# Moving the weight tiles of an fp32r transformer trunk to another SBUF offset

## The chip, the cores and the metric

The kernel runs on one core of one Trainium2 chip. The metric is device time in microseconds. Times of several executions are given as their median. The profile comes from one execution of its own.

## The reference

The reference computes a trunk of two layers on 256 tokens with 1024 features, all in float32. Cut to what matters:

```python
for i in range(DEPTH):                                    # DEPTH = 2
    x = x + 0.5 * swiglu(rms_norm(x, ffn1_norm_g[i]), ffn1_w_in[i], ffn1_w_out[i])
    hn = rms_norm(x, mix_norm_g[i])
    if i % 2 == 0:                                        # mixer 0: mLSTM heads
        proj = hn @ a_w_in[0]
        y_tok = mlstm_heads(proj[..., :A_TOK], a_gate_b[0], a_h_norm_g[0])
    else:                                                 # mixer 1: sliding-window heads
        proj = hn @ b_w_in[0]
        y_tok = swa_heads(proj[..., :B_TOK], cos, sin, ...)
    y_mem = memory_heads(proj[..., TOK:], mem_k, mem_v, ...)   # cross-attention to 256 memory rows
    x = x + concat([y_tok, y_mem], -1) @ w_out
    x = x + 0.5 * swiglu(rms_norm(x, ffn2_norm_g[i]), ffn2_w_in[i], ffn2_w_out[i])

def swiglu(x, w_in, w_out):                               # hidden width 2816
    gate, up = jnp.split(x @ w_in, 2, axis=-1)
    return (jax.nn.silu(gate) * up) @ w_out
```

Before the layers, memory keys and values are computed as `rms_norm(mem) @ mem_w_kv`. So there are four feed-forward blocks, two mixers and a memory part; nearly all arithmetic is in products with weight matrices.

## The kernel before

Activations are kept transposed, features on the 128 partitions and the 256 tokens along a row. Each weight matrix is read once from HBM in tiles of 128 partitions by 1024 float32 values (`wtile`: pool `wrp`, tile `wr`, 5 buffers, issued on the SyncE queue). For the precision, each operand is split into a part rounded to fp32r and the rest: ScalarE writes the rounded part of the weights (`wh`, pool `whp`, 8 buffers), VectorE the rest (`wl`, pool `wlp`, 8 buffers). The split activations are the tiles `xh` and `xl` (pools `xhp`, `xlp`, 4 buffers each, two feature chunks per tile, written by `Norm.put`) for a norm's output, and tiles `u` (pool `up`) for hidden units, head outputs and the memory rows. The helper `mm3` (lines 227 to 229) makes one product out of three matmuls, high by high, high by low and low by high, all added up in one PSUM bank.

There are two arrangements. In the feed-forward blocks (`ffn_in`, `ffn`), in the output projections of the mixers (`out_proj`) and in a part of the first mixer's input projection, a 128x128 piece of a weight tile stands in the array (it is loaded by an LDWEIGHTS, the profile's engine PEld) and 256 columns of activations move through it. In groups with `rows=True` (the memory part, six groups of the first mixer and all seven of the second) it is the other way round: 128 columns of an activation tile stand and 256 columns of a weight tile move. The memory part also has a first stretch of its own (`first_part`, line 357). Every matmul is preceded by its own load.

Which tile of a pool is used next, and at which address each pool lies, follows from the order in which the pools are made: pools are placed one after another along each partition's row of SBUF, and a pool's size shifts all that come after it. A tile's begin modulo 512 bytes is called its residue here. The pieces within a tile lie 512 or 1024 bytes apart, so a whole tile has one residue. In the built program before:

| tiles | first address | residue |
|---|---|---|
| kT, vM (memory keys, values) | 20416 | 448 |
| xh, xl | 29120, 37312 | 448 |
| u | 45504 | 448 |
| wr, wh, wl | 113152, 133632, 166400 | 0 |
| t (scratch) | 199168 | 0 |
| acc | 218368 | 256 |
| onesr (constant, for the sums of a norm) | 16512 | 128 |

The order of the work on TensorE and on the SyncE queue is written out by hand: generators for the main chain and for the side chains of norms and heads are woven by the class `Weave` by a table of expected delays (`LAT`), and only these two engines are kept to that order. The other engines are scheduled by the framework. `memory()` starts with 18 matmuls on a zeroed scratch tile, while the first transfers are under way.

The five norms are made in `program()`. `x1` feeds the first mixer, `x4` the second; `x0`, `x2`, `x3` and `x5` feed the feed-forward blocks. `x4` is the only one all of whose products have it standing.

Of the kernel before, what the change touches and what calls it, by code (L numbers as in the profile page):

```python
# [10 lines left out]
F32 = mybir.dt.float32  # L11
F32R = mybir.dt.float32r
# [7 lines left out]
P = 128  # L20
T = 256
# [27 lines left out]
G_MEM, G_F1, G_MIX, G_F2, G_XQ, G_XK, G_AH, G_BQ, G_BK, G_END = 0, 8, 24, 40, 56, 58, 60, 68, 69, 70  # L49
# [49 lines left out]
def tile_trunk(ctx: ExitStack, tc: tile.TileContext, a, out):  # L99
    nc = tc.nc  # L100
    seq = [0]

    def mk(pool, shape, dt, tag):
        seq[0] += 1
        return pool.tile(shape, dt, tag=tag, name=f"{tag}_{seq[0]}")

    def pool(name, bufs, **kw):
        return ctx.enter_context(tc.tile_pool(name=name, bufs=bufs, **kw))
# [7 lines left out]
    xhp = pool("xhp", 4)  # L116
    xlp = pool("xlp", 4)
    up = pool("up", 31)
    vp = pool("vp", 2)
    wrp = pool("wrp", 5)  # L120
    whp = pool("whp", 8)
    wlp = pool("wlp", 8)
# [78 lines left out]
    def g(i):  # L201
        return gcol[:, i:i + 1]
# [38 lines left out]
    def split_gain(src, gc, hi, lo):  # L241
        act(hi, src, AF.Copy, scale=gc)
        nc.vector.scalar_tensor_tensor(out=lo, in0=src, scalar=gc, in1=hi.bitcast(F32),
                                       op0=ALU.mult, op1=ALU.subtract)
# [9 lines left out]
    class Norm:  # L254


        def __init__(self, gi, rows=True, half=True, cols=False):
            self.gi, self.rows, self.half, self.cols, self.rc = gi, rows, half, cols, None
            self.done = False
            self.xT, self.xh, self.xl = [], [], []  # L260

        def put(self, xn):
            c2 = len(self.xT)
            hi, lo = mk(xhp, [P, 2, T], F32R, "xh"), mk(xlp, [P, 2, T], F32R, "xl")
            for m in range(2):
                split_gain(xn[:, m], g(self.gi + 2 * c2 + m), hi[:, m], lo[:, m])
            self.xh.append(hi)
            self.xl.append(lo)
            self.xT.append(xn)
            self.square(xn, c2 == 0)  # L270
            if c2 == 3:
                self.fold()
# [732 lines left out]
    def program():  # L1005
        yield from memory()
        x1, x2, x3 = Norm(G_MIX, half=False, cols=True), Norm(G_F2), Norm(G_F1 + 8)
        x4, x5 = Norm(G_MIX + 8, rows=False), Norm(G_F2 + 8)
        yield from ffn(x0, a["ffn1_w_in"][0], a["ffn1_w_out"][0], x1, late_constants)
        yield from mixer_a(x1, x2)  # L1010
        yield from ffn(x2, a["ffn2_w_in"][0], a["ffn2_w_out"][0], x3)
        yield from ffn(x3, a["ffn1_w_in"][1], a["ffn1_w_out"][1], x4, rope_tables)
        yield from mixer_b(x4, x5)
        yield from ffn(x5, a["ffn2_w_in"][1], a["ffn2_w_out"][1])

    with tc.manual_schedule(engines={mybir.EngineType.PE, mybir.EngineType.SP}):
        wv.run(program())
# [38 lines left out]
```

## Time and profile before

| | |
|---|---|
| time, median of 3 runs | 1009.38 us (1009.06 to 1010.25) |
| profiled execution, its own time | 1010.58 us |
| its span (first to last instruction) | 1008.7 us |
| mean granted TensorE clock | 0.996 |
| TensorE matmuls in the span | 8560 |
| HBM read | 180.32 MB |

The profile names an instruction by its line, its engine and its operands: `bank<-xh,wh` is a matmul that writes a PSUM bank, with the moving operand first and the standing one second. A group's row gives the count, the busy time, the mean duration of one in nanoseconds and the idle time of the engine ahead of it. A matmul's duration contains the way through the array and overlaps with the next two; how fast matmuls follow one another is seen from their count in a window.

### The profile page before, as it was taken

What the parts mean: (1) busy time and instruction counts of PE and PEld (TensorE: products, weight loads), DVE (VectorE), ACT (ScalarE), POOL (GpSimd) and SP (SyncE); (2) the same over time, 40 slices, a digit from 0 to 9 for tenths busy, and PEclk for the clock granted to TensorE, in tenths of its full rate; (3) what the DMA queues carried; (4) which work ended last, traced back from release to release, by engine and by line L of the source; (5) the groups of instructions that cost most, each with busy time, mean ns of one, the idle gap of its engine ahead of it and who ended that gap; (6) DMA issues with size and microseconds to landing.
All of it is one profiled execution on the core that took longest, in us unless ns stands there. A gap on an engine that the chain in (4) does not pass through costs nothing.

```text
span 1008.7 us, 20573 instructions
## 1 busy us (share of the span) xinstructions
PE 996.2 (99%) x8560; PEld 978.1 (97%) x8560; DVE 664.4 (66%) x1078; ACT 531.0 (53%) x779; POOL 29.7 (3%) x27
## 2 busy tenths in 40 slices
PE   8899999999999999999999999999999999999998
PEld 6899999999999999999999999999997899999998
DVE  6776665668766696666567665656777768666551
ACT  7654444446566464444445444455578755454440
POOL 1100000000100000000000000000132000000000
PEclk9999999999999999999999999999999999999999
DMA  9676656676634666665666666556641257666550
GB/s 307 197 250 197 195 180 195 185 190 194 189 126 136 185 191 199 190 195 180 198 193 201 201 192 191 186 180 200 205 148 50 88 157 223 193 192 187 187 168 22
DMA packets 173204, 182.70 MB, mean 181 GB/s; under 512 B 7124, under 2 KB 168328, under 8 KB 173112
## 3 DMA queue, kind: packets, MB, share of 16 engines
q1 hardware_dynamic: 171872, 179.60, 58.1%
q10 hardware_dynamic: 1016, 1.58, 0.5%
q8 instruction: 67, 1.10, 0.4%
q0 software_dynamic: 224, 0.22, 0.2%
q14 instruction: 25, 0.20, 0.1%
HBM read 180.32 MB, written 1.05 MB: 180 GB/s over the span
## 4 chain that ended last, share of the span: by engine, by line
PE 94%; ACT 2%; DVE 2%; DMA 1%; issue 0%; SPq 0%; POOL 0%; ACTq 0%; DVEq 0%
PE bank L227 30%; PE bank L229 30%; PE bank L228 30%; PE bank L233 2%; ACT u L134 1%; PE bank L238 1%; DMA wr<-in_mem_w_kv_dram 1%; DVE wl L214 1%; ACT wh L213 1%; PE bank L989 1%; DVE col L957 0%; PE bank L303 0%; DVE col L956 0%; SPq L435 0%; DVE u L248 0%
## 5 line engine op out<-in xcount | busy, mean ns | idle before, releaser
L214 DVE TENSOR_TENSOR wl<-wr,wh 128x1024 fp32r<-128x1024 f32 (+1 forms) x347 | 414.6, 1197 | 273.1 <-ACT wh L213 272.0
L213 ACT CAST wh<-wr 128x1024 fp32r<-128x1024 f32 (+1 forms) x347 | 356.7, 1032 | 389.8 <-PE bank L228 364.9
L227 PE MATMUL bank<-xh,wh 128*128 128x256 f32 x1544 | 427.8, 277 | 0.0
L228 PE MATMUL bank<-xl,wh 128*128 128x256 f32 x1544 | 426.4, 276 | 0.0
L229 PE MATMUL bank<-xh,wl 128*128 128x256 f32 x1544 | 426.4, 276 | 0.0
L227 PEld LDWEIGHTS bank<-xh,wh 128*128 128x128 f32 x1544 | 290.0, 188 | 0.1
L228 PEld LDWEIGHTS bank<-xl,wh 128*128 128x128 f32 x1544 | 289.9, 188 | 0.1
L229 PEld LDWEIGHTS bank<-xh,wl 128*128 128x128 f32 x1544 | 289.9, 188 | 0.0
L227 PE MATMUL bank<-u,wh 128*128 128x256 f32 x896 | 249.3, 278 | 0.0
L228 PE MATMUL bank<-u,wh 128*128 128x256 f32 x896 | 247.6, 276 | 0.0
L229 PE MATMUL bank<-u,wl 128*128 128x256 f32 x896 | 247.5, 276 | 0.0
L227 PEld LDWEIGHTS bank<-u,wh 128*128 128x128 f32 x896 | 168.2, 188 | 1.7 <-issue 1.7
L228 PEld LDWEIGHTS bank<-u,wh 128*128 128x128 f32 x896 | 168.3, 188 | 0.1
L229 PEld LDWEIGHTS bank<-u,wl 128*128 128x128 f32 x896 | 168.2, 188 | 0.0
L227 PE MATMUL bank<-wh,xh 128*128 128x256 f32 x208 | 59.6, 287 | 0.4 <-ACT t L982 0.4
L228 PE MATMUL bank<-wl,xh 128*128 128x256 f32 x208 | 57.9, 278 | 0.0
L229 PE MATMUL bank<-wh,xl 128*128 128x256 f32 x208 | 57.8, 278 | 0.0
L501 DVE TENSOR_TENSOR t<-bank,rb 128x256 f32<-128x256 f32 x88 | 36.4, 421 | 6.7 <-PE bank L229 6.7
L227 PEld LDWEIGHTS bank<-wh,xh 128*128 128x128 f32 x208 | 39.1, 188 | 1.1 <-ACT t L982 0.7
L228 PEld LDWEIGHTS bank<-wl,xh 128*128 128x128 f32 x208 | 39.0, 188 | 0.1
L229 PEld LDWEIGHTS bank<-wh,xl 128*128 128x128 f32 x208 | 39.0, 188 | 0.0
L134 ACT ACTIVATE u<-bank,col,col 128x256 f32<-128x256 f32 (+1 forms) x48 | 24.9, 530 | 15.2 <-DVE col L960 7.9
(180 smaller groups left out, 682.9 us busy)
## 6 DMA issues: line engine op xcount, KB each, us to landing
wr<-in_ffn_w_in_dram SPq DMA_DIRECT2D x176, 512.0 KB, 4.4
wr<-in_ffn_w_out_dram SPq DMA_DIRECT2D x80, 512.0 KB, 4.0
wr<-in_a_w_in_dram SPq DMA_DIRECT2D x28, 512.0 KB, 3.9
wr<-in_b_w_in_dram SPq DMA_DIRECT2D x14, 512.0 KB, 4.5
wr<-in_a_w_out_dram SPq DMA_DIRECT2D x12, 512.0 KB, 3.3
wr<-in_b_w_out_dram SPq DMA_DIRECT2D x12, 512.0 KB, 3.3
wr<-in_ffn_w_out_dram SPq DMA_DIRECT2D x16, 256.0 KB, 2.7
wr<-in_mem_w_kv_dram SPq DMA_DIRECT2D x7, 512.0 KB, 7.8
```

What stands on the lines that cost most here:

```text
L134: ins = nc.scalar.activation(*args, **kw)
L213: last[0] = nc.scalar.copy(hi[:, i * n:(i + 1) * n], src[:, i * n:(i + 1) * n])
L214: tt(out=lo[:, i * n:(i + 1) * n], in0=src[:, i * n:(i + 1) * n], in1=hi[:, i * n:(i + 1) * n].bitcast(F32), op=ALU.subtract)
L227: nc.tensor.matmul(ps, wh, xh, start=start, stop=False, skip_group_check=True)
L228: nc.tensor.matmul(ps, wh, xl, start=False, stop=False, skip_group_check=True)
L229: nc.tensor.matmul(ps, wl, xh, start=False, stop=stop, skip_group_check=True)
L233: nc.tensor.matmul(ps, lhsT, rhs, start=start, stop=stop, skip_group_check=True)
L238: nc.tensor.transpose(ps, src, ident[:k, :k])
L501: tt(out=t[:, m], in0=ps[m][:, :T], in1=x.rb, op=ALU.mult)
L989: nc.tensor.matmul(o[es[e], cs], vr[:, i, js], pTs[e][:, src], start=i == 0, stop=i == 1, skip_group_check=True)
```

## The change

A tile of 128x112 float32 values (448 bytes in each partition) is made in a pool of its own between the pools `vp` and `wrp`; two columns of it are set to zero once, and it isn't read. All pools behind it move. The tiles `xh` and `xl` become 512 bytes longer and are used from column `at` on; `at` is 0 for all norms but `x4`, where it is 16 columns, 64 bytes.

```diff
     up = pool("up", 31)
     vp = pool("vp", 2)
+    gap = mk(pool("gap", 1), [P, 112], F32, "gap")
+    nc.vector.memset(gap[:, :2], 0.0)
     wrp = pool("wrp", 5)
...
-        def __init__(self, gi, rows=True, half=True, cols=False):
+        def __init__(self, gi, rows=True, half=True, cols=False, at=0):
+            self.at = at
...
         def put(self, xn):
             c2 = len(self.xT)
-            hi, lo = mk(xhp, [P, 2, T], F32R, "xh"), mk(xlp, [P, 2, T], F32R, "xl")
+            hi, lo = (mk(p, [P, 2 * T + P], F32R, tag)[:, self.at:self.at + 2 * T].rearrange("p (m t) -> p m t", m=2)
+                      for p, tag in ((xhp, "xh"), (xlp, "xl")))
...
         x1, x2, x3 = Norm(G_MIX, half=False, cols=True), Norm(G_F2), Norm(G_F1 + 8)
-        x4, x5 = Norm(G_MIX + 8, rows=False), Norm(G_F2 + 8)
+        x4, x5 = Norm(G_MIX + 8, rows=False, at=16), Norm(G_F2 + 8)
```

In the built program the residues become 448 for wr, wh, wl and t, and 192 for acc; xh, xl and u stay at 448, except that x4's xh and xl are read from residue 0. For the fp32r matmuls this means:

| place | moving, standing before | moving, standing after |
|---|---|---|
| feed-forward, output projections, part of the first mixer | 448, 0 | 448, 448 |
| memory part, six groups of the first mixer | 0, 448 | 448, 448 |
| second mixer's input projection | 0, 448 | 448, 0 |

The order of instructions is the same on TensorE, ScalarE, GpSimd and the SyncE queue. On VectorE one memset is added at the start. Before, the first rows of VectorE (onesr, ones, mhalf are constants; t is the zeroed scratch tile of the first matmuls):

```order
L1052 UNCONDITIONAL_BRANCH
L112 MEMSET onesr_58 128x128
L172 MEMSET ones_114 128x1
L174 MEMSET mhalf_116 128x16
L428 MEMSET t_133 128x256
```

And with the change:

```order
L1056 UNCONDITIONAL_BRANCH
L112 MEMSET onesr_58 128x128
L121 MEMSET gap_75 128x2
L174 MEMSET ones_119 128x1
L176 MEMSET mhalf_121 128x16
L432 MEMSET t_138 128x256
```

The memset of `gap` stands ahead of the three others; nothing else moved. Line numbers in the changed kernel are higher by 2 from there on, and by 4 behind `Norm.put`.

## The prediction

> **What bounds the kernel now.** I read the page's busy times, then its chain that ended last, then the windows.
>
> ```profile
> PE 996.2 (99%) x8560; PEld 978.1 (97%) x8560; DVE 664.4 (66%) x1078; ACT 531.0 (53%) x779; POOL 29.7 (3%) x27
> PE 94%; ACT 2%; DVE 2%; DMA 1%; issue 0%; SPq 0%; POOL 0%; ACTq 0%; DVEq 0%
> L227 PE MATMUL bank<-xh,wh 128*128 128x256 f32 x1544 | 427.8, 277 | 0.0
> L227 PE MATMUL bank<-u,wh 128*128 128x256 f32 x896 | 249.3, 278 | 0.0
> L227 PE MATMUL bank<-wh,xh 128*128 128x256 f32 x208 | 59.6, 287 | 0.4 <-ACT t L982 0.4
> L227 PE MATMUL bank<-wh,u 128*128 128x256 f32 x56 | 17.4, 310 | 2.6 <-ACT wh L213 2.6
> ```
>
> TensorE carries 94% of the chain. In a matmul's name the moving operand stands first, the stationary one (loaded by PEld) second. Three such groups belong to each product of `mm3`, so weights are stationary in 3 x (1544 + 896) = 7320 matmuls and activations in 3 x (208 + 56) = 792, and 24 more from line 357. The change alters no row of TensorE's order; it can act on 99% of the span only through the time that one matmul takes to follow another. That time I take from the windows (columns: window, its length, PE busy and matmuls in it, PEclk, DMA share, GB/s):
>
> ```profile
> 47.00:226.00 179.00, 179.00 (x1582) 1.00 0.66 200
> 342.00:700.00 358.00, 358.00 (x3161) 1.00 0.63 193
> 816.00:1004.00 188.00, 188.00 (x1661) 1.00 0.55 168
> ```
>
> A window counts also the matmuls under way at its left edge, so its length plus one duration (0.276 us) over its count is the pitch: 358.276 / 3161 = 113.3 ns, and 179.276 / 1582 and 188.276 / 1661 give the same. These are the four feed-forward blocks, 6404 matmuls in 725 us, about 6397 without the edges. The granted clock is 1.00 there. Elsewhere there is a second pitch:
>
> ```profile
> 294.00:301.50 7.50, 7.50 (x66) 7.50 (x65) 3.78 (x4) 4.31 (x6) 0.00 (x0) 1.00 0.51 168
> 328.00:334.00 6.00, 6.00 (x53) 6.00 (x52) 5.68 (x30) 4.21 (x11) 0.70 (x1) 1.00 0.57 167
> 714.00:722.50 8.50, 8.50 (x78) 8.50 (x77) 7.57 (x11) 5.13 (x8) 0.00 (x0) 1.00 0.74 231
> 723.50:731.50 8.00, 8.00 (x70) 8.00 (x69) 6.57 (x21) 4.43 (x8) 2.95 (x3) 1.00 0.59 185
> ```
>
> PE is never idle in these four, yet the first gives 7.776 / 66 = 117.8 ns, and the second and fourth 118.4 and 118.2 (coarser, by their small counts), while the third, also with weights as the moving operand, gives 8.776 / 78 = 112.5, the usual pitch within one count. So one and the same arrangement of operands runs at a **short pitch** (113.3) or a **long pitch** (117.8, 4.4 ns more). The long one holds until something disturbs it. A matmul's own duration shows which of the two it runs at (columns: count, busy us, mean ns; first two rows from 294 to 301.5 us, the next from 328 to 334, the last from 714 to 722.5):
>
> ```profile
> L228 PE MATMUL bank<-wl,xh 128*128 128x256 f32 x22 | 6.2, 280 | 0.0
> L229 PE MATMUL bank<-wh,xl 128*128 128x256 f32 x22 | 6.1, 279 | 0.0
> L229 PE MATMUL bank<-u,wl 128*128 128x256 f32 x18 | 5.1, 281 | 0.0
> L229 PE MATMUL bank<-wh,xl 128*128 128x256 f32 x26 | 7.2, 276 | 0.0
> ```
>
> 276 goes with the short pitch, 279 to 281 with the long.
>
> **The change, part by part.** *Gap memset.* One 128x2 memset more on VectorE, ahead of the one of tile t that the first matmul waits for.
>
> ```profile
> 0.95 0.06 DVE L172 MEMSET ones<- 128x1 f32 x1
> 1.04 0.27 DVE L428 MEMSET t<- 128x256 uint32 x1
> 1.37 6.74 PE L431 MATMUL bank<-t 128*128 128x512 bf16 x18 [1.37 <-DVE t L428]
> 3.62 7.27 DMA wr<-in_mem_w_kv_dram
> ```
>
> It costs 0.06 us at most. The 18 matmuls only fill the wait for the first weights, whose transfer is on the chain of waits until 10.9 us (last row), so I take 0; without that cover it is 0.06.
>
> *Other engines' tiles.* wr, wh, wl and t move too, so casts, subtractions and transfers see new addresses. Rows with different residues already agree: t at 0 with acc at 256, and t at 0 with u at 448.
>
> ```profile
> L281 DVE TENSOR_TENSOR acc<-acc,t 128x512 f32<-128x512 f32 x21 | 14.4, 687 | 0.2
> L248 DVE TENSOR_TENSOR u<-t,u 128x512 fp32r<-128x512 f32 x44 | 30.1, 684 | 0.0
> L214 DVE TENSOR_TENSOR wl<-wr,wh 128x1024 fp32r<-128x1024 f32 (+1 forms) x347 | 414.6, 1197 | 273.1 <-ACT wh L213 272.0
> ```
>
> I take 0, between plus and minus 3 ns on 687. TensorE's queue covers it: VectorE is idle 273 us ahead of the subtraction. Without that cover, 3 / 687 of 414.6 us would be 1.8 us.
>
> *The feed-forward matmuls.* Before, a weight load reads at residue 0 while the matmul in front streams activations at residue 448. Afterwards both are at 448. No steady stretch of before has this; single pairs do, where the program passes from weights that stand to activations that stand. There an activation at 448 is loaded under a matmul that streams activations at 448. The timeline at one such place, and then the row of that one matmul from windows at 245.70, 290.28 and 713.53 us:
>
> ```profile
> 245.68 0.28 PE L229 MATMUL bank<-xh,wl 128*128 128x256 f32 x1
> 245.69 0.19 PEld L227 LDWEIGHTS bank<-wh,xh 128*128 128x128 f32 x1
> ...
> L229 PE MATMUL bank<-xh,wl 128*128 128x256 f32 x1 | 0.3, 277 | 0.0
> L229 PE MATMUL bank<-xh,wl 128*128 128x256 f32 x1 | 0.3, 278 | 0.0
> L229 PE MATMUL bank<-u,wl 128*128 128x256 f32 x1 | 0.3, 277 | 0.0
> L227 PE MATMUL bank<-xh,wh 128*128 128x256 f32 x2 | 0.6, 276 | 0.0
> L303 PE MATMUL bank<-u,onesr 128*128 128x256 f32 x2 | 0.4, 276 | 0.0
> ```
>
> The load of xh starts 0.01 us after the matmul that streams xh. 277, 278, 277 against 276. The last two rows (363.5 to 363.9 us) are the control: there the constant onesr, at residue 128, is loaded under activations at 448, and nothing grows. The long pitch has rows of 279 to 281, so equal residues lie between the two. I charge the excess to every matmul, (1 + 2 + 1) / 3 = 1.33 ns: 6397 x 1.33 = **+8.5 us**. Bounds: 0, if such a pair costs only where the operands change roles; 4.4 ns, if equal residues lock the long pitch in, which is 6397 x 4.4 = +28.1 us.
>
> The Trainium skill (TensorE: Matmul & The Clock Gate, Step-by-step: what each phase is for) says that TensorE has two independent read ports and that loading the next weights doesn't steal bandwidth from the running matmul; by it this term would be 0 and the time that of before. The matmuls at 277 and 278 speak weakly against it, the two pitches at one arrangement more.
>
> *The mixers and the memory part.* Their rows, from 246 to 336 us (first three) and from 714 to 813:
>
> ```profile
> L228 PE MATMUL bank<-wl,xh 128*128 128x256 f32 x96 | 26.7, 278 | 0.0
> L228 PE MATMUL bank<-xl,wh 128*128 128x256 f32 x64 | 17.9, 279 | 0.0
> L228 PE MATMUL bank<-u,wh 128*128 128x256 f32 x43 | 12.0, 279 | 0.0
> L228 PE MATMUL bank<-wl,xh 128*128 128x256 f32 x112 | 31.2, 278 | 0.0
> L228 PE MATMUL bank<-u,wh 128*128 128x256 f32 x61 | 17.0, 278 | 0.0
> ```
>
> With 276 for the short pitch and some 280 to 281 for the long one, about half of these have the long one, and the mean is near 115.6. At equal residues they would go to 113.3 + 1.3 = 114.7: the 7320 - 6397 = 923 with standing weights gain 0.9 ns each (-0.8 us), the first mixer's 96 x 3 = 288 with standing activations another -0.3. The memory part's 192 (56 x 3 + 24) I take at the long pitch, since its rows are the longest: 3.1 ns each, -0.6. Bounds for all of these: everything at the short pitch, 923 x 2.3 + 288 x 2.3 + 192 x 4.4 = -3.6 us; everything at the long one, 1211 x 2.2 = +2.7.
>
> *The second mixer's norm.* Its 112 x 3 = 336 matmuls change places: weights stream at 448, activations stand at 0. That is what the same mixer's output projection has today, and its row reads 278 as well: 0, between -0.8 (336 x 2.3) and +0.7.
>
> **Sum**: 8.5 - 0.8 - 0.3 - 0.6 = +6.8 us. The profiled execution took 1010.58 us (span 1008.7 and 1.9 around it) and gives 1017.4; it is 1.2 us over the median of the runs shown, 1009.38, so on that scale I predict **1016.2**.
>
> **The rivals.** *A, addresses don't matter to the feed-forward matmuls* (faster or no change). Their pitch of 113.3 is the same to 0.1 ns in all four blocks and occurs, from 714 to 722.5 us, with the residues the other way round; the pair costs were seen only where the roles change. Then only mixers and memory count: between -3.6 - 0.8 = -4.4 and +3.4 us. The gain comes only if equal residues return to the short pitch more readily than today; I centre it at -1.7, 1007.7. Against it stand the three rows above.
>
> *B, the long pitch locks in* (slower still). From 294 to 301.5 us nothing leads back to 113.3; if a feed-forward block enters at the long pitch and equal residues keep it there, each block costs about a quarter of 28.1, 7 us, and all four with the mixers' +2.7 give 1040. It decides at the entry of each block. Against it: 277 is not 280.
>
> *C, a lower pitch* (faster). Some part of 113.3 may itself be a collision that equal residues avoid. Transposes show that less is possible with a load between any two:
>
> ```profile
> 334.64 0.60 PE L238 MATMUL bank<-con,t 128*128 128x128 f32 x4
> L238 PE MATMUL bank<-con,t 128*128 128x128 f32 x24 | 3.6, 272 | 0.0
> ```
>
> (0.60 - 0.272) / 3 = 0.109 us; at 109 ns the blocks would save 6397 x 4.3 = 27.5 us, 982. Against it: in three pairs the matmul got longer, in none shorter.
>
> By the Trainium skill (same page, Back-to-back issue gap) an isolated matmul of 256 columns takes 256 / 2.4 + 2.5 = 109.2 ns, an estimate from its formula; the trace's 113.3 is above it, and by the formula alone the blocks would come out at C's time.
>
> *D, nothing moves*: the pools might round the gap away. The built program's addresses say that they don't.
>
> **How the numbers follow.** My forecast 0.38, A 0.36, B 0.14, C 0.10, D 0.02. A measurement of this kernel tells about 0.2%, 2.0 us, from no change. The forecast and B are slower (0.51, with 0.01 left for a forecast that comes out too small to see). A is faster by over 2.0 us about as often as not (0.17; no change 0.18; slower 0.01), C faster (0.10), D no change. That makes faster 0.27, no change 0.21, slower 0.52. The forecast's own range is 1012 to 1022 (0.7 to 2 ns per matmul, mixers as above). The whole range, 1005 to 1034, holds A almost to its lower bound and B up to three blocks, and leaves out C and the end of B.
>
> **What would show it.** In the profile after, the windows from 47 to 226, 342 to 700 and 816 to 1004 us tell it alone: a pitch near 114.7 with matmul rows at 277 to 278 is my forecast, 113.3 with 276 is A, 117.8 with 280 or more B, below 113 C. The second mixer's rows with wl moving should stay near 278. If the blocks keep 113.3 and the mixers' rows fall to 276, I have taken the cost of changing roles for the cost of equal residues. I am wrong altogether if the time moves and the pitch doesn't.

## The result, and the profile after

The changed kernel takes 1057.18 us (median of 4 runs, 1056.86 to 1058.59), the kernel before 1009.82 (4 runs, 1009.06 to 1010.8): ratio 1.0471, interval 1.0458 to 1.0483. The profiled execution took 1057.12 us, its span is 1055.3. So the change costs 47 us; the prediction was 1016.2 with a range of 1005 to 1034. It was slower, as forecast, but by 47 us instead of 7 and outside the range.

The page of the changed kernel (busy times, the chain that ended last, and the costliest groups; lines behind `Norm.put` have numbers higher by 4, those ahead of it by 2):

```profile
PE 1042.6 (99%) x8560; PEld 1024.6 (97%) x8560; DVE 664.8 (63%) x1079; ACT 529.5 (50%) x779; POOL 29.7 (3%) x27
PE 96%; ACT 1%; DVE 1%; DMA 1%; SPq 0%; issue 0%; POOL 0%; DVEq 0%; ACTq 0%
L216 DVE TENSOR_TENSOR wl<-wr,wh 128x1024 fp32r<-128x1024 f32 (+1 forms) x347 | 414.7, 1196 | 312.1 <-ACT wh L215 310.2
L229 PE MATMUL bank<-xh,wh 128*128 128x256 f32 x1544 | 438.2, 284 | 0.0
L229 PE MATMUL bank<-u,wh 128*128 128x256 f32 x896 | 255.2, 285 | 0.0
```

TensorE's busy time went from 996.2 to 1042.6 us, 46.4 of the 46.6 us by which the span grew. The other engines work as long as before and only wait longer: VectorE is idle 312.1 us ahead of its subtraction instead of 273.1, and one takes 1196 ns instead of 1197. A matmul lasts 284 ns where it lasted 277.

The windows of the changed kernel over the feed-forward blocks (columns: window, length, PE busy and matmuls, PEld, DVE, ACT, POOL, PEclk, DMA share, GB/s):

```profile
46.00:234.00 188.00, 188.00 (x1569) 188.00 (x1568) 116.28 (x150) 87.57 (x104) 0.00 (x0) 1.00 0.62 189
360.00:735.00 375.00, 375.00 (x3127) 375.00 (x3127) 232.26 (x308) 176.29 (x215) 0.00 (x0) 1.00 0.59 182
860.00:1050.00 190.00, 190.00 (x1586) 190.00 (x1585) 109.00 (x146) 79.11 (x96) 0.00 (x0) 1.00 0.50 159
```

Read as in the prediction (length plus one matmul over the count): 375.283 / 3127 = 120.0 ns, and 120.0 in the other two. That is neither the short pitch (113.3) nor the long one (117.8): equal residues have **a third pitch, 120.0**, at a granted clock of 1.00 and with no idle time. 6397 x (120.0 - 113.33) = +42.7 us. Counted from the matmuls' starts in the trace, stretches with equal residues outside the blocks also run at 119.5 to 120.0, which adds some 5.5 us. The input projection of the second mixer, the one place with unequal residues, falls from 116.5 to 115.2 (-0.4 us). Together that is about 48 of 46.6; the memory part took 1.2 us less in its waits for transfers and other engines.

The second mixer, in the changed kernel's groups from 753 to 847 us:

```profile
L230 PE MATMUL bank<-wl,xh 128*128 128x256 f32 x101 | 28.1, 278 | 0.0
L230 PE MATMUL bank<-u,wh 128*128 128x256 f32 x60 | 16.9, 282 | 0.0
```

The first row (weights move at 448, activations stand at 0) reads 278 as before. The second, the same mixer's output projection, now has both at 448 and went from 278 to 282.

**Where the third pitch sets in.** The timeline of the changed kernel's TensorE, where the norm's two matmuls with onesr stand in a feed-forward block:

```profile
378.20 0.28 PE L230 MATMUL bank<-xl,wh 128*128 128x256 f32 x1
378.32 0.28 PE L231 MATMUL bank<-xh,wl 128*128 128x256 f32 x1
378.44 0.39 PE L307 MATMUL bank<-u,onesr 128*128 128x256 f32 x2
378.66 0.28 PE L229 MATMUL bank<-xh,wh 128*128 128x256 f32 x1
378.78 0.28 PE L230 MATMUL bank<-xl,wh 128*128 128x256 f32 x1
378.90 0.28 PE L231 MATMUL bank<-xh,wl 128*128 128x256 f32 x1
```

Starts lie 0.12 us apart, but the two onesr matmuls take 0.22 together: 113 and 114 ns by the trace's starts, the short pitch, for onesr (128) is loaded under activations at 448. It comes one matmul late: the matmul at 378.32, under which onesr is first loaded, still lasts 283 ns and has 121 behind it. Then comes the return. The groups of the same kernel from 378.82 to 378.92 us:

```profile
L229 PE MATMUL bank<-xh,wh 128*128 128x256 f32 x1 | 0.3, 283 | 0.0
L307 PE MATMUL bank<-u,onesr 128*128 128x256 f32 x1 | 0.3, 278 | 0.0
```

Under the second onesr matmul a weight tile at 448 is loaded while activations at 448 stream, the first equal pair after unequal ones. That matmul lasts 278 ns and the next follows after 114. Under the matmul behind it (283 ns) the second equal pair runs, and only there the gap is 119, and 120 from then on. The other feed-forward blocks (53.24, 568.74 and 871.06 us) and the first mixer (240.67 us) show the same within 1 ns. One could think that the price of each pair merely comes one matmul late. The kernel before speaks against that: behind the matmuls of its single equal pairs (245.68, 290.26 and 713.52 us) the gaps are 114 and 115 ns and then 113 again, some 2 ns in all. So a single equal pair shows 277 or 278 ns and hardly any delay. The full price appears at the second in a row, and the places from which the prediction took its rows have no two in a row.

### The profile page after: what moved, and what is told of

It is laid out like the page before. It is cut to its first block, busy times and chain, and to the rows that moved or that the text cites. A ratio compares the mean times of both kernels' runs of the same rounds, so it can differ in the third digit from the quotient of the medians.

```text
span 1055.3 us, 20574 instructions
## 1 busy us (share of the span) xinstructions
PE 1042.6 (99%) x8560; PEld 1024.6 (97%) x8560; DVE 664.8 (63%) x1079; ACT 529.5 (50%) x779; POOL 29.7 (3%) x27
## 4 chain that ended last, share of the span: by engine, by line
PE 96%; ACT 1%; DVE 1%; DMA 1%; SPq 0%; issue 0%; POOL 0%; DVEq 0%; ACTq 0%
PE bank L229 31%; PE bank L230 31%; PE bank L231 31%; PE bank L235 2%; PE bank L240 1%; DMA wr<-in_mem_w_kv_dram 1%; ACT u L136 1%; PE bank L993 1%; ACT wh L215 0%; DVE wl L216 0%; PE bank L956 0%; PE bank L307 0%; PE bank L951 0%; DVE col L961 0%; SPq L439 0%
## 5 line engine op out<-in xcount | busy, mean ns | idle before, releaser
L216 DVE TENSOR_TENSOR wl<-wr,wh 128x1024 fp32r<-128x1024 f32 (+1 forms) x347 | 414.7, 1196 | 312.1 <-ACT wh L215 310.2
L229 PE MATMUL bank<-xh,wh 128*128 128x256 f32 x1544 | 438.2, 284 | 0.0
L231 PE MATMUL bank<-xh,wl 128*128 128x256 f32 x1544 | 436.9, 283 | 0.0
L230 PE MATMUL bank<-xl,wh 128*128 128x256 f32 x1544 | 436.9, 283 | 0.0
L230 PEld LDWEIGHTS bank<-xl,wh 128*128 128x128 f32 x1544 | 296.4, 192 | 0.1
L229 PEld LDWEIGHTS bank<-xh,wh 128*128 128x128 f32 x1544 | 296.4, 192 | 0.1
L231 PEld LDWEIGHTS bank<-xh,wl 128*128 128x128 f32 x1544 | 296.4, 192 | 0.0
L229 PE MATMUL bank<-u,wh 128*128 128x256 f32 x896 | 255.2, 285 | 0.0
L230 PE MATMUL bank<-u,wh 128*128 128x256 f32 x896 | 253.5, 283 | 0.0
L231 PE MATMUL bank<-u,wl 128*128 128x256 f32 x896 | 253.5, 283 | 0.0
L229 PEld LDWEIGHTS bank<-u,wh 128*128 128x128 f32 x896 | 171.9, 192 | 1.7 <-issue 1.7
L230 PEld LDWEIGHTS bank<-u,wh 128*128 128x128 f32 x896 | 171.9, 192 | 0.1
L508 DVE TENSOR_TENSOR t<-t,bank 128x256 f32<-128x256 f32 x88 | 32.7, 413 | 0.0
```

The costliest lines, as they stand in the source:

```text
L216: tt(out=lo[:, i * n:(i + 1) * n], in0=src[:, i * n:(i + 1) * n], in1=hi[:, i * n:(i + 1) * n].bitcast(F32), op=ALU.subtract)
L229: nc.tensor.matmul(ps, wh, xh, start=start, stop=False, skip_group_check=True)
L230: nc.tensor.matmul(ps, wh, xl, start=False, stop=False, skip_group_check=True)
L231: nc.tensor.matmul(ps, wl, xh, start=False, stop=stop, skip_group_check=True)
L508: tt(out=t[:, m], in0=t[:, m], in1=ps[m][:, T:], op=ALU.mult)
```

## The experiments

In all of them, "difference" is the residue of the tile being loaded minus that of the tile streaming meanwhile, modulo 512. Before, the feed-forward blocks have 64 (w 0, activations 448), after the change 0. Only e11 and e12 were timed repeatedly, the others give one time. The kernel before took 1009.28 us beside e1 to e4, 1010.72 beside e5 to e8, 1009.11 (median of 15) beside e9 to e11 and 1009.9 (of 7) beside e12 and e13.

**e1, both at 0.** The kernel before without the gap, all norm outputs at residue 0. So xh, xl against w have difference 0 at another residue than in the changed kernel, while u against w keeps 64. (`x0` is made ahead of `memory()`, so its edit stands apart.)

```diff
-    x0 = Norm(G_F1)
+    x0 = Norm(G_F1, at=16)
...
+        x1, x2, x3 = Norm(G_MIX, half=False, cols=True, at=16), Norm(G_F2, at=16), Norm(G_F1 + 8, at=16)
+        x4, x5 = Norm(G_MIX + 8, rows=False, at=16), Norm(G_F2 + 8, at=16)
```

> Weights at residue 0 as before, and the activations of every norm (xh, xl of x0 to x5) at residue 0 too; hidden units and head outputs (u) stay at 448. So the first products of the feed-forward blocks (4 x 1056 = 4224 matmuls) and the input projections of both mixers have equal residues, both 0, while the second products of the feed-forward blocks keep 448 moving over 0. Theory R (it is the difference of the two residues that sets the pitch, and difference 0 gives 120 ns): 120 ns in the first products, 113.3 in the second; 4224 x 6.7 = 28 us, and the mixers' 288 + 408 + 336 matmuls with some 4.4 ns each 4.5 us: 1009.8 + 33 = 1042 us. Rival S (a standing piece of 512 bytes that begins at 448 lies across a multiple of 512 and loads more slowly, whatever moves): 113.3 in both, 1008 to 1010 us.

Measured 1040.9 us. Two windows of e1, the first products of one block and its second products:

```profile
374.00:489.00 115.00, 115.00 (x961) 115.00 (x960) 71.35 (x98) 52.63 (x62) 0.00 (x0) 1.00 0.58 187
490.00:548.00 58.00, 58.00 (x514) 58.00 (x513) 34.77 (x40) 27.43 (x35) 0.00 (x0) 1.00 0.61 194
```

115.283 / 961 = 120.0 for 0 against 0, and 58.276 / 514 = 113.4 for u at 448 against 0. That is theory R's 1042 us within 1.2; rival S, a standing piece that is slow by its own place, falls. What costs here is the relation of the two tiles, not where either lies.

**e2, e3, e4: other gaps.** The gap is 192, 64 or 448 bytes, and x4 is at column 0 in all three, so e4 is the change without its second part.

```diff
-    gap = mk(pool("gap", 1), [P, 112], F32, "gap")
+    gap = mk(pool("gap", 1), [P, 48], F32, "gap")
...
-        x4, x5 = Norm(G_MIX + 8, rows=False, at=16), Norm(G_F2 + 8)
+        x4, x5 = Norm(G_MIX + 8, rows=False), Norm(G_F2 + 8)
```

(48 columns for e2, 16 for e3, 112 for e4.)

> Gap of 192 bytes: weights at residue 192, all activations at 448, difference 256 whichever of the two stands. Theory R: 113.3 ns in the feed-forward blocks, as with differences 64 and 192; if a difference as far as this one also keeps the mixers and the memory part at 113.3, up to 3.6 us less than before, 1006 to 1010 us. Rival S (a standing piece across a multiple of 512 is slow): 120 ns in the feed-forward blocks, 1055 to 1058 us. Rival P (the period is 256 bytes and not 512): 120 ns everywhere, 1058 us.

> Gap of 64 bytes: weights at residue 64, all activations at 448, standing minus moving 128 with weights standing and 384 with activations standing. Theory R: 113.3 ns in the feed-forward blocks, 1007 to 1011 us. A rival by which the cost falls off with the distance gives something between 113.3 and 120 if 64 was only just far enough. Rival S: 120 ns, 1055 to 1058 us. One earlier sight of difference 128 (a matmul with weights at 0 over the load of a constant at 128) was followed by the pitch of 117.8: a third theory has 117.8 here, 1036 to 1040 us.

> The gap alone: as the changed kernel, but the second mixer's norm stays at residue 448 like the others, so its 336 matmuls with standing activations have equal residues. Theory R: 120 ns there instead of a mix of 113 and 118 (mean near 115.4): 336 x 4.6 = +1.5 us on 1057.2, 1058.7 us. If the offset of that norm does nothing: 1057 us.

Measured 1058.33, 1054.99 and 1059.91 us. One window of each, in this order:

```profile
379.00:568.00 189.00, 189.00 (x1577) 189.00 (x1576) 115.58 (x152) 87.11 (x105) 0.00 (x0) 1.00 0.59 186
```

```profile
378.00:567.00 189.00, 189.00 (x1578) 189.00 (x1577) 115.94 (x152) 86.96 (x105) 0.00 (x0) 1.00 0.59 186
```

```profile
379.00:568.00 189.00, 189.00 (x1577) 189.00 (x1577) 116.00 (x152) 87.08 (x105) 0.00 (x0) 1.00 0.58 187
```

All three are at 120 in these windows (189.283 / 1577 = 120.0). In e2 the difference is 256, in e3 128. The idea that only equality modulo 512 costs, by which e2 and e3 should have kept 113.3, was a miss twice. e3 differs in kind: its gaps scatter between 115 and 123 ns, with a mean near 120 in three blocks and 118.7 in the third. e4 is 2.7 us above the changed kernel. Its second mixer has both at 448 and a pitch of 119.7 instead of 115.2, which makes that stretch 1.4 us longer. Another 1.5 us lie in the memory part, whose residues are the same in both kernels, so they aren't the edit's; every other stretch is equal to 0.02 us. So nearly the whole loss is the gap's; placing x4 elsewhere saved a little of it.

**e5, e6, e7: 128, 32 and 480.** The same edit with gaps of 32, 8 and 120 columns (differences 192, 96 and 32).

```diff
-    gap = mk(pool("gap", 1), [P, 112], F32, "gap")
+    gap = mk(pool("gap", 1), [P, 32], F32, "gap")
```

> Gap of 128 bytes: weights at residue 128, activations at 448; standing minus moving is 192 with weights standing, 320 with activations standing. The runs so far: differences 0, 256 and 128 (384 the other way) have 119.5 to 120 ns, 64 (448 the other way) 113.3 with stretches of 117.8. Theory Q (only the difference modulo 128 counts: an even number of 64-byte steps is long, an odd one short): 113.3 ns in the feed-forward blocks, mixers as before, 1006 to 1011 us. Theory R in its first form (a period of 512 with a short pitch only next to 64): 119 to 120, 1052 to 1058 us.

> Gap of 32 bytes: weights at residue 32, activations at 448; difference 96 with weights standing, 416 with activations standing, half way between a short and a long one. Theory Q with a step (what counts is in which 64-byte half each operand begins): 96 lies in the same step as 64, 113.3 ns, 1007 to 1011 us. Theory Q with a slope (the two reads drift into each other): between, some 116 to 117 ns, 1025 to 1040 us. If the pitch falls below 113.3, half steps are the best place: below 1005 us.

> Gap of 480 bytes: weights at residue 480, difference 32 with weights standing, 480 with activations standing: the half step on the other side of 64. Theory Q with a step that rounds down (32 belongs to 0): 120 ns, 1055 to 1059 us; with a slope, between, 1025 to 1040 us; symmetric about 64 (as the run at 96): the same pitch as there.

Measured 1039.59, 1048.57 and 1046.89 us. Windows of e5, then one of e6 and one of e7:

```profile
343.00:735.00 392.00, 392.00 (x3331) 392.00 (x3330) 245.60 (x322) 187.00 (x227) 0.00 (x0) 1.00 0.59 186
```

```profile
380.00:560.00 180.00, 180.00 (x1520) 180.00 (x1519) 109.59 (x142) 84.69 (x102) 0.00 (x0) 1.00 0.59 185
```

```profile
380.00:560.00 180.00, 180.00 (x1524) 180.00 (x1523) 110.08 (x142) 85.10 (x102) 0.00 (x0) 1.00 0.59 186
```

392.281 / 3331 = 117.8 for e5: the long pitch, in every block from its first matmul to its last. 180.28 / 1520 = 118.6 and 180.28 / 1524 = 118.3 for the other two, at gaps that scatter. No expectation had 1039.59: theory Q's 113.3 and theory R's 119 to 120 both missed the blocks of e5. In its second mixer, though, where activations stand (difference 320), e5 runs at 113.3 by the starts from 735.7 to 744.7 us, ahead of the onesr matmuls. With before and after, that gives a pattern. Even numbers of 64-byte steps (0, 128, 256) cost about 120. Odd ones run at 113.3 (64 before, 320 in e5) or at 117.8 (192 in e5), and the next runs show both at the same difference: a matmul of odd difference has two steady pitches. Half steps lie irregularly between; of what was expected of e6 and e7 only the likeness of the two held, roughly.

**e8: weights 448, norm outputs 384.** A difference of 64 again for the first products of each block, as before the change, but at other addresses; the second products stay at 0.

```diff
-    x0 = Norm(G_F1)
+    x0 = Norm(G_F1, at=112)
...
+        x1, x2, x3 = Norm(G_MIX, half=False, cols=True, at=112), Norm(G_F2, at=112), Norm(G_F1 + 8, at=112)
+        x4, x5 = Norm(G_MIX + 8, rows=False, at=112), Norm(G_F2 + 8, at=112)
```

> Weights at 448 as in the changed kernel, and the activations of all norms at residue 384: difference 64 again in the first products of the feed-forward blocks (4224 matmuls), while the second products keep 448 over 448. Theories R and Q: the first products return to 113.3 ns, the second stay at 120; 1057.2 - 4224 x 6.67 ns = 1029 us, and a few us less or more in the mixers' input projections (standing activations at difference 448): 1025 to 1030 us. Rival S (a standing piece that begins at 448 is slow in itself): 1057 us.

Measured 1044.66 us. Three windows of e8: the first products of one block up to the norm's onesr matmuls, the rest of them, and the second products:

```profile
364.50:373.30 8.80, 8.80 (x80) 8.80 (x79) 8.80 (x14) 7.50 (x11) 0.00 (x0) 1.00 0.36 114
374.00:488.00 114.00, 114.00 (x970) 114.00 (x969) 72.46 (x100) 52.88 (x62) 0.00 (x0) 1.00 0.60 192
490.00:551.00 61.00, 61.00 (x510) 61.00 (x510) 34.18 (x40) 26.99 (x33) 0.00 (x0) 1.00 0.56 182
```

9.076 / 80 = 113.5, 114.281 / 970 = 117.8, 61.283 / 510 = 120.2. Rival S falls again, but 1025 to 1030 us was a miss: only a part of each block returned to 113.3. The block begins at the short pitch, goes over to the long one exactly at the onesr matmuls (it is knocked over, as it is called below) and stays. onesr (128) is loaded there under activations at 384, a difference of 256, and the next weight tile under the norm's sums at 448, a difference of 0. In the kernel before these are 192 and 64, and nothing happens.

**e9: only onesr moved.** This is the direct test of that reading, on the kernel before.

```diff
-    onesr = mk(cst, [P, P], F32R, "onesr")
+    onesr = mk(cst, [P, 2 * P], F32R, "onesr")[:, 16:16 + P]
```

> The kernel before, with one thing changed: the constant onesr begins at residue 192 instead of 128 (its tile is 1024 bytes long, so everything behind it moves by 512 and keeps its residue). It is loaded 14 times in all, under activations that stream at residue 448: the difference is 256, an even number of 64-byte steps, where it was 320, an odd one. Weights stay at 0 and activations at 448. Theory Q with memory (even differences cost at once; after one of them the matmuls of odd difference behind it go on at the long pitch, 117.8, until something else disturbs them): each feed-forward block falls to 117.8 at its norm's onesr matmuls, some 80 matmuls in, and stays there: about 6000 x 4.4 ns = +26 us, 1036 us. Rival (the pitch follows from the difference of the two operands that run, and nothing is remembered): the 14 matmuls cost 0.1 us, 1009 to 1010.5 us and 113.3 ns in the blocks.

Measured 1037.52 us. Windows of e9 ahead of the onesr matmuls of one block, behind them, and over the next block:

```profile
342.00:369.50 27.50, 27.50 (x245) 27.50 (x244) 20.37 (x29) 16.35 (x25) 0.00 (x0) 1.00 0.52 163
370.00:556.00 186.00, 186.00 (x1582) 186.00 (x1581) 116.34 (x153) 87.35 (x105) 0.00 (x0) 1.00 0.60 190
557.00:733.00 176.00, 176.00 (x1497) 176.00 (x1496) 107.83 (x141) 82.75 (x98) 0.00 (x0) 1.00 0.59 185
```

27.776 / 245 = 113.4, then 186.281 / 1582 = 117.8 and 176.281 / 1497 = 117.8. Moving the operand of 14 matmuls by 64 bytes costs 28 us, since the 6000 matmuls behind them keep the pitch into which they were knocked. The third block has the long pitch from its first matmul on, since the second one ends in it. The rival without memory (1009 to 1010.5) falls. That all tiles behind onesr also moved by 512 bytes is not the cause: in e11 they moved by 1024, and its blocks run at 113.3 as before.

**e10: odd differences around onesr.** e8 with onesr at 192 and the norm's sums at 256, in a pool of their own.

```diff
-            self.sums = unit(F32R)
+            self.sums = mk(smp, [P, 2, T], F32R, "u")
```

> e8 (weights 448, norm outputs 384, other activations 448: first products of each feed-forward block at an odd difference, second products at an even one) with the onesr of residue 192 and the sums that it is multiplied with at 256, so that onesr and what stands around it have odd differences (192 - 384, 192 - 256, 448 - 256). Theory Q with memory: nothing knocks the first products any more, all of them run at 113.3 and not only the first 80 of each block; 3864 matmuls x 4.45 ns = 17.2 us less than e8's 1044.7, so 1027.5 us. Rival (e8's 117.8 came from where the block stands or from its transfers, not from onesr): 1044 to 1045.

Measured 1038.14 us: a miss. The blocks behave as in e8. Windows of e10 ahead of and behind the onesr matmuls:

```profile
357.50:366.30 8.80, 8.80 (x80) 8.80 (x79) 8.80 (x14) 7.50 (x12) 0.00 (x0) 1.00 0.35 112
367.00:481.00 114.00, 114.00 (x971) 114.00 (x970) 72.47 (x100) 52.76 (x62) 0.00 (x0) 1.00 0.61 192
```

Again 113.5, then 117.7. So an odd difference alone doesn't protect. The loads at that place have the differences 320, 448, 192. The groups of e10 from 366.62 to 366.70 us:

```profile
L308 PE MATMUL bank<-u,onesr 128*128 128x256 f32 x1 | 0.3, 279 | 0.0
L232 PE MATMUL bank<-xh,wl 128*128 128x256 f32 x1 | 0.3, 276 | 0.0
```

The last matmul ahead of onesr, under which 320 runs, still has 276 ns; the first onesr matmul, under which 448 runs, already 279. The 6.5 us less than e8 come from elsewhere; e12 is about them.

**e13: e10 with the sums at 384.** The differences become 320, 320, 64.

```diff
-            self.sums = mk(smp, [P, 2, T], F32R, "u")
+            self.sums = mk(smp, [P, 2 * T + 32], F32R, "u")[:, 32:].rearrange("p (m t) -> p m t", m=2)
```

> e10 with the sums at residue 384 instead of 256. Around onesr the differences of load and running stream are then 320, 320, 64 where e10 had 320, 448, 192; both sets are odd numbers of 64-byte steps, both come from 64 and go back to 64. In e10 the matmul under which the difference was 448 was the first that grew (279 ns), the one before it, under 320, had 276. Theory Q' (the step from 320 to 448 knocks, and 320 itself fits the short pitch): the first products of all four blocks stay at 113.3 and the whole is 3864 x 4.45 ns = 17 us below e10's 1038.1, near 1021 us. Rival Q'' (any change of the difference out of 64 other than the kernel before's to 192 knocks, 320 too): 1037.5 to 1039 us.

Measured 1021.57 us, as theory Q' had it. Two windows of e13, all first products of a block with the onesr matmuls among them, and the second products:

```profile
354.00:473.00 119.00, 119.00 (x1052) 119.00 (x1051) 81.63 (x113) 60.54 (x73) 0.00 (x0) 1.00 0.62 193
475.00:536.00 61.00, 61.00 (x511) 61.00 (x510) 34.40 (x40) 26.93 (x34) 0.00 (x0) 1.00 0.58 183
```

119.276 / 1052 = 113.4 through the whole stretch, and 119.9 behind it. So weights at 448 are as good as weights at 0, if the activations under which they are loaded stand at 384 and nothing in the block knocks them.

**e11: the second mixer at 320.** The kernel before with x4 at residue 320, its sums at 0 and a second copy of the ones at 64.

```diff
+    onesr, onesb = ones2[:, :P], ones2[:, 240:240 + P]
...
+            self.sums = mk(tp, [P, 2, T], F32R, "t") if self.at else unit(F32R)
...
+        x4, x5 = Norm(G_MIX + 8, rows=False, at=96), Norm(G_F2 + 8, at=0)
```

> The kernel before with the standing activations of the second mixer's norm at residue 320, that norm's sums at residue 0 and a second copy of the ones for it at residue 64; all else as before. Theory Q with memory: the second mixer's 336 matmuls with standing activations, at a mean of 116.2 ns before, have an odd difference and nothing that knocks them, so they run at 113.3: -1.0 us, 1008.5 to 1009.5 us; a little less if something in the mixer still knocks them. Rival (differences of 64 and 320 aren't the same, or the mixer's other products decide): no difference, or up to +1 us.

Measured 1010.72 us, ratio 1.0003 (0.9992 to 1.0013): no difference, a miss. A window of e11 over the beginning of the second mixer:

```profile
713.00:731.00 18.00, 18.00 (x155) 18.00 (x154) 14.66 (x32) 10.55 (x17) 2.98 (x3) 1.00 0.63 199
```

18.28 / 155 = 117.9 from the first matmul. The kernel before runs at 113 here until it comes to onesr (723.16 us), which knocks it over (differences 128, 192, 0). In e11 the entry itself knocks: x4 at 320 is first loaded under activations at 448, a difference of 384. In the kernel before that one pair has the difference 0, and the short pitch survives it.

**e12: only a pool for the sums.** The kernel before, all residues that TensorE reads as they were.

```diff
+    smp = pool("smp", 1)
     pb8 = pool("pb8", 8, space=PSUM)
...
-            self.sums = unit(F32R)
+            self.sums = mk(smp, [P, 2 * T + 32], F32R, "u")[:, 32:].rearrange("p (m t) -> p m t", m=2)
```

> The kernel before, every address that TensorE reads at its old residue, but the sums of the norms in a tile of a pool of their own (residue 448 too) in place of one of the 31 u tiles. In e10, which had such a pool, the memory part ended 6.5 us earlier than in e8: ScalarE cast two weight tiles ahead of the scaling that waits for the norm's rc, where before and in e8 it waited with the casts queued behind it, and TensorE stood idle near 30 us. The built program has that new order on ScalarE here as well. Theory: the first 46 us shrink by some 6 us and everything behind runs as before, at 113.3 ns: 1002.5 to 1004.5 us. Rival (e10's early start came from its addresses, or is lost again at the first feed-forward block, which then waits for its weights): 1007 to 1010 us.

Measured 1003.77 us, ratio 0.9941 (0.9925 to 0.9958): 0.6% less than the kernel before, small but clear of its interval. ScalarE's timeline in the kernel before and in e12:

```profile
24.27 0.58 ACT L134 ACTIVATE t<-bank 128x512 f32<-128x512 f32 x1
24.75 0.50 ACT L134 ACTIVATE xh<-u,gcol 128x256 fp32r<-128x256 f32 x1
29.46 0.84 ACT L134 ACTIVATE vM<-bank,rc 128x256 f32<-128x256 f32 x2 [4.21 <-POOL rc L308]
30.20 1.04 ACT L213 CAST wh<-wr 128x1024 fp32r<-128x1024 f32 x1
```

```profile
23.62 1.98 ACT L214 CAST wh<-wr 128x1024 fp32r<-128x1024 f32 x2
25.51 0.59 ACT L135 ACTIVATE t<-bank 128x512 f32<-128x512 f32 x1
26.00 1.03 ACT L214 CAST wh<-wr 128x1024 fp32r<-128x1024 f32 x1
30.27 0.84 ACT L135 ACTIVATE vM<-bank,rc 128x256 f32<-128x256 f32 x2 [3.24 <-POOL rc L309]
```

Before, ScalarE waits 4.21 us for the norm's rc with the next weight cast queued behind the waiting row. In e12 three casts stand ahead of it. The windows from 28 to 34 us of before and of e12 show what TensorE makes of it:

```profile
28.00:34.00 6.00, 2.54 (x20) 2.14 (x19) 5.10 (x14) 4.54 (x7) 2.08 (x2) 1.00 0.00 0
```

```profile
28.00:34.00 6.00, 6.00 (x53) 6.00 (x52) 5.44 (x12) 3.73 (x6) 2.64 (x2) 1.00 0.64 176
```

It is busy 6.00 of 6 us instead of 2.54. Everything behind starts some 5 us earlier, at nearly unchanged pitches (the last block's last matmul starts at 999.4 instead of 1004.6 us; the first block alone changed, by 0.3 us). So this gain isn't one of pitch. It comes with the order that the framework's scheduler gives ScalarE when the sums no longer take one of the 31 u tiles.

## Why the prediction was right and wrong

**What bounds the kernel, and where the change acts:** right. TensorE is 96% of the chain, its busy time carries the whole difference, and the three windows named for it tell it alone.

**The gap memset and the other engines' tiles, 0:** right. The memset takes 0.06 us beside the others, the subtraction 1196 ns against 1197.

**The feed-forward matmuls, 1.33 ns each:** the step that failed. The mechanism was right, equal residues slow every matmul (e2 and e3 show that they are only one case of it); the term was mis-sized by a factor of five and measured 6.67 ns, +42.7 us instead of +8.5. It was sized by single pairs, at which the equal residues last for one load. The changed kernel shows that the first equal load after unequal ones costs about what those rows showed (278 ns, next gap 114) and the second in a row the full price (283 ns, gap 119 and then 120). The rows read in the kernel before have no second one, so none of them could size this term.

**Its upper bound, 4.4 ns:** wrong too. It took the long pitch for the worst that a matmul can have, and 277 to 278 ns for a place between the two pitches. Equal residues have a pitch of their own above both, 120.0, with 283 ns. The long pitch is the second steady pitch of an odd difference, as e5 and e9 show.

**The rule of the Trainium skill weighed there** (TensorE: Matmul & The Clock Gate, Step-by-step: what each phase is for) says that loading the next weights doesn't steal bandwidth from the running matmul. As a rule for the time, the measurement decides against it: the same instructions at the same clock run at 113.3, 117.8 or 120.0 ns depending on where the two tiles lie to each other and, at odd differences, on what ran before.

**The mixers and the memory part, -1.7 us:** wrong in sign, since it follows from the same 1.33. At equal residues these too run at 119.5 to 120.0, some +5.5 us.

**The second mixer's norm, 0:** right (278 before and after; by starts 116.5 to 115.2, -0.4 us).

**The rivals:** A (addresses don't matter) and C (a lower pitch) are refuted by the windows of the changed kernel, and A by e1 as well. D falls with the time. B was nearest with its 1040, but by another way: the blocks don't fall into the long pitch, they leave both. Its mechanism exists all the same, and e9 shows it at 1037.5 us.

**Not settled:** what decides between 113.3 and 117.8 at an odd difference. Starting from the short pitch, these loads left it in place: 192, 192, 64 (kernel before); 320, 320, 64 (e13); 192, 192, 448 (e8, second mixer); one load of 0 (before, into the mixers). These knocked it over: 256, 256, 64 (e9); 256, 192, 0 (e8); 320, 448, 192 (e10); 128, 192, 0 (before, second mixer); one load of 384 (e11). So in these runs the short pitch was lost whenever one of the differences around onesr was even, but e10 shows that odd ones alone can end it too. There are ways back as well. A stretch at 120 was followed by the short pitch in e8 and e1, within five matmuls. In e12 the first block falls into the long pitch at its transposes (near 39.8 us), and the loads 192, 192, 64 at onesr bring it back at 48.5 us. The lists are facts; a rule that covers them was not found. What inside the chip collides was not tested either.

## What to carry to other kernels

Where TensorE is the bound and each matmul loads a new stationary tile, look at the start addresses of the two tiles relative to each other. Here a difference of an even number of 64-byte steps cost up to 5.9% of every matmul, and a pad costs next to nothing (the memset of `gap` took 0.06 us). Measure it on a steady stretch, from counts in a window: a single pair told a fifth of the price. And look at the few other matmuls in between, since 14 of them set the pitch of 6000.

## What the runs showed of the hardware that was not expected

- The pitch of fp32r matmuls with 256 moving columns depends on the two tiles' relative start in SBUF: 120.0 ns at differences of 0 and 256, near 120 and scattered at 128, 113.3 or 117.8 at 64, 117.8 at 192, 118.3 to 118.6 on average at 32 and 96 (all with weights standing, at a granted clock of 1.00).
- In the pairs tried, the difference of the residues counts and not the residues themselves: 0 against 0 and 448 against 448 both give 120.0, 0 against 448 and 448 against 384 both 113.3.
- At an odd difference the pitch has a memory: after one disturbance 1500 matmuls in a row stayed at 117.8 (e9) that run at 113.3 without it.
- A difference of 0 sets in over two matmuls, with gaps of 114 and then 119 to 120 ns (after the onesr matmuls of the changed kernel). It goes away one matmul late there (121, then 113), and over three in e8 (behind the matmuls from 364.03 us on: 121, 121, 116, then 114).
